# Max-unpooling on one core: inputs and outputs in three sections of whole images, six loads in place of three

## The chip, the cores and the metric

The kernel runs on one core of one Trainium2 chip. The metric is the device time in microseconds of one execution. Ten executions of the kernel before gave a median of 71.7 us, from 71.55 to 71.92. A profiled execution also has a span, from its first recorded instruction to its last.

## The reference

Each input pixel goes to one of the four places of its 2x2 block in an output of twice the height and width; the index, 0 to 3, says which. The other three are zero.

```python
# x: (16, 64, 32, 32) float32; indices: the same shape, values 0..3; kernel_size 2
output = np.zeros((batch, channels, 64, 64), dtype=np.float32)
for b, c, i, j in every position of x:
    idx = indices[b, c, i, j]
    output[b, c, 2 * i + idx // 2, 2 * j + idx % 2] = x[b, c, i, j]
```

(The loop is written in one line here.) On the chip the indices are 64-bit integers in HBM, so that x is 4.19 MB, the indices 8.39 MB and the output 16.78 MB.

## The kernel before, in words

There are 1024 images (batch times channels) of 1024 pixels. Each of the 128 partitions takes eight neighbouring images, `T = 8`. Input and output tiles are laid out by partition: a partition's x is 32 KB in one piece of HBM, its indices 64 KB, its output 128 KB.

Three loads are issued on SP's queue: all of x (L109), then the indices of images 0 to 2 of each partition (24 KB per partition) and those of images 3 to 7 (40 KB; both L112). `Program.first` takes each out of the place where it was made and puts it just ahead of SP's first drain, which is ahead of the barrier at which the engines start together. One semaphore per load tells VectorE of its arrival.

VectorE does all the arithmetic with one kind of instruction (L133): for each of the four places of a block it compares the low 32-bit word of the index (every second word of the tile) with 0, 1, 2 or 3, multiplies the outcome by x, and writes with a step of two pixels in each direction into the output tile. Four such instructions make one or two images per partition. The waits are at L117 (x) and L122 (indices, ahead of images 0 and 3). One or two images are done at a time: 0 and 1, 2, 3, 4 and 5, 6 and 7.

The output goes out in four groups of two images per partition, each 4.19 MB (L146): in HBM a store is 128 pieces of 32 KB, one per partition, 128 KB apart. SP waits for VectorE's count `made`, issues the store, and goes to the next. There are three output tiles; the fourth group uses the first tile again, so that VectorE waits for the first store (L128) ahead of it. At the end of the program SP waits for the other three stores (L151).

All transfers go through one queue in the order of their issue: three loads, then four stores.

Of the kernel before, what the change touches and what calls it, by code (L numbers as in the profile page):

```python
# [1 line left out]

# [4 lines left out]

P = 128
F32 = mybir.dt.float32
I32 = mybir.dt.int32  # L10


class Program:

    def __init__(self, nc):
        self.nc = nc
        self.block = nc.main_func.blocks[0]  # L20
        self.kernel_block = nc.cur_bb.bb.name

    def __enter__(self):
        ins = self.block.instructions
        self.branches = [i for i in ins if "Branch" in type(i).__name__]
        n = len(ins) - len(self.branches)
        assert all("Branch" in type(ins[k]).__name__ for k in range(n, len(ins)))
        del ins[n:]
        self.nc.switch_bb(self.block.name, parent=None)
        self.symbolic = self.nc._always_lower_symbolic_ap  # L30
        self.nc._always_lower_symbolic_ap = False
        return self

    def first(self, made):
        ins = self.block.instructions
        assert ins[len(ins) - 1].name == made.ins.name
        moved = ins.pop()
        at = next(
            k
            for k, i in enumerate(ins)  # L40
            if i.engine == moved.engine and isinstance(i, mybir.InstDrain)
        )
        ins.insert(at, moved)

    def last(self, made):


        def move(nc):
            ins = self.block.instructions
            at = next(k for k, i in enumerate(ins) if i.name == made.ins.name)  # L50
            nc.main_func.blocks[-1].instructions.append(ins.pop(at))

        self.nc.at_finalize(move)

    def __exit__(self, kind, *_):
        self.nc._always_lower_symbolic_ap = self.symbolic
        if kind is None:
            for b in self.branches:
                self.block.instructions.append(b)
            self.nc.switch_bb(self.kernel_block, parent=None)  # L60


@with_exitstack
def kernel(
    ctx: ExitStack,
    tc: tile.TileContext,
    x: bass.AP,
    indices: bass.AP,
    kernel_size: bass.AP,
    out: bass.AP,  # L70
):
    nc = tc.nc
    assert kernel_size == 2

    B, C, H, W = x.shape
    n_img = B * C
    T = n_img // P
    assert T * P == n_img and C % T == 0

    G = 2  # L80
    NG = T // G
    FIRST = 3
    N = H * W
    x_v = x.rearrange("b (ch t) h w -> (b ch) (t h w)", t=T)
    idx_v = indices.rearrange("b (ch t) h w -> (b ch) (t h w)", t=T).bitcast(I32)
    out_v = out.rearrange("b (ch g t) oh ow -> g (b ch) (t oh ow)", g=NG, t=G)

    x_t = nc.alloc_sbuf_tensor("x_t", [P, T * N], F32).ap()
    idx_t = nc.alloc_sbuf_tensor("idx_t", [P, T * 2 * N], I32).ap()
    out_t = [  # L90
        nc.alloc_sbuf_tensor(f"out_t{g}", [P, G * 4 * N], F32).ap()
        for g in range(NG - 1)
    ]
    out_t.append(out_t[0])

    x_in = nc.alloc_semaphore("x_in")
    idx_in = [nc.alloc_semaphore(f"idx_in{g}") for g in range(2)]
    made = nc.alloc_semaphore("made")
    stored_0 = nc.alloc_semaphore("stored_0")
    stored = nc.alloc_semaphore("stored")  # L100

    x_c = x_t.rearrange("p (t i j) -> p t i j", t=T, j=W)
    idx_c = idx_t.rearrange("p (t i j two) -> p t i j two", t=T, j=W, two=2)[
        :, :, :, :, 0
    ]
    cut = FIRST * 2 * N

    with Program(nc) as program:
        program.first(nc.sync.dma_start(out=x_t, in_=x_v).then_inc(x_in, 16))  # L109
        for half, part in enumerate((slice(0, cut), slice(cut, None))):  # L110
            program.first(
                nc.sync.dma_start(out=idx_t[:, part], in_=idx_v[:, part]).then_inc(  # L112
                    idx_in[half], 16
                )
            )

        nc.vector.wait_ge(x_in, 16).then_inc(x_in, -16)  # L117
        for t in range(T):
            g, k = t // G, t % G
            if t in (0, FIRST):  # L120
                half = int(t == FIRST)
                nc.vector.wait_ge(idx_in[half], 16).then_inc(idx_in[half], -16)  # L122

            if k == 1 and t != FIRST:
                continue
            n = 1 if k == 1 or t + 1 == FIRST else 2
            if g == NG - 1:
                nc.vector.wait_ge(stored_0, 16).then_inc(stored_0, -16)  # L128
            o_c = out_t[g].rearrange(
                "p (m i two j wo) -> p m i two j wo", m=G, two=2, wo=2, j=W  # L130
            )
            for pidx in range(4):
                op = nc.vector.scalar_tensor_tensor(  # L133
                    out=o_c[:, k : k + n, :, pidx // 2, :, pidx % 2],
                    in0=idx_c[:, t : t + n],
                    scalar=pidx,
                    in1=x_c[:, t : t + n],
                    op0=mybir.AluOpType.is_equal,
                    op1=mybir.AluOpType.mult,
                )  # L140
            if k + n == G:
                op.then_inc(made, 1)

        for g in range(NG):
            nc.sync.wait_ge(made, g + 1)
            nc.sync.dma_start(out=out_v[g], in_=out_t[g]).then_inc(  # L146
                stored if g else stored_0, 16
            )
        nc.sync.sem_inc(made, -NG)
        program.last(  # L150
            nc.sync.wait_ge(stored, 16 * (NG - 1)).then_inc(stored, -16 * (NG - 1))  # L151
        )


# [1 line left out]
_INS = ['x', 'indices', 'kernel_size']  # L156
_OUTS = [((16, 64, 64, 64), 'float32')]

_NUMBERS = {'kernel_size': 2}


# [26 lines left out]
```

## Time and profile before

| What | Value |
|---|---|
| Median of ten executions | 71.7 us |
| The profiled execution | 71.78 us |
| Its span | 70.5 us |
| VectorE busy | 35.6 us, 20 instructions |
| Of these, 128x2048 | 12, of 2287 ns each |
| Of these, 128x1024 | 8, of 1220 ns each |
| First VectorE instruction of L133 | at 19.75 us |
| SP's issue of the loads | 0.37 us (x), 0.90 us for the two of the indices |
| First and last store issued | at 28.7 and 55.4 us |
| Moved by DMA | 29.36 MB in 1008 packets |

A "packet" is what one DMA engine records as one piece of work. The 1008 are seven transfers on 16 engines with nine packets each: eight of data and a last one of four bytes that counts up the semaphore. The time from issue to landing counts the wait behind earlier transfers of the queue. The profile's chain of work that ended last goes through the engines' instructions; transfers are not steps of it. Lines are those of the kernel printed above.

### The profile page before, as it was taken

What the parts mean: (1) busy time and instruction counts of PE and PEld (TensorE: products, weight loads), DVE (VectorE), ACT (ScalarE), POOL (GpSimd) and SP (SyncE); (2) the same over time, 40 slices, a digit from 0 to 9 for tenths busy, and PEclk for the clock granted to TensorE, in tenths of its full rate; (3) what the DMA queues carried; (4) which work ended last, traced back from release to release, by engine and by line L of the source; (5) the groups of instructions that cost most, each with busy time, mean ns of one, the idle gap of its engine ahead of it and who ended that gap; (6) DMA issues with size and microseconds to landing.
All of it is one profiled execution on the core that took longest, in us unless ns stands there. A gap on an engine that the chain in (4) does not pass through costs nothing.

```text
span 70.5 us, 72 instructions
## 1 busy us (share of the span) xinstructions
DVE 35.6 (51%) x20; POOL 0.2 (0%) x4
## 2 busy tenths in 40 slices
DVE  0000000000079999999999999999999400000000
POOL 1000000000000000000000000000000000000000
DMA  9779796999988999969899897979798998979790
GB/s 260 316 335 539 335 558 274 446 446 446 581 372 372 395 558 488 419 298 521 372 465 428 353 540 316 558 335 539 335 521 372 465 428 353 540 316 558 335 539 37
DMA packets 1009, 29.36 MB, mean 417 GB/s; under 512 B 113, under 2 KB 113, under 8 KB 113
## 3 DMA queue, kind: packets, MB, share of 16 engines
q1 hardware_dynamic: 1008, 29.36, 97.5%
q14 instruction: 1, 0.00, 0.0%
HBM read 12.58 MB, written 16.78 MB: 417 GB/s over the span
## 4 chain that ended last, share of the span: by engine, by line
DVE 46%; DVEq 4%; issue 1%
DVE out_t L133 46%; DVEq L183 4%
## 5 line engine op out<-in xcount | busy, mean ns | idle before, releaser
L133 DVE SCALAR_TENSOR_TENSOR out_t<-idx_t,x_t 128x2048 f32<-128x2048 int32 (+1 forms) x20 | 35.6, 1860 | 19.8 <-DVEq L122 19.8
L169 POOL MEMSET const-bfloat16-1.0<- 128x1 bf16 x1 | 0.1, 101 | 0.0
L169 POOL MEMSET const-uint8-127<- 128x1 uint8 x1 | 0.1, 101 | 0.0
L169 POOL MEMSET const-float32-0.0<- 128x1 f32 x1 | 0.1, 98 | 0.2 <-issue 0.2
L169 POOL MEMSET const-float32-1.0<- 128x1 f32 x1 | 0.1, 98 | 0.0
## 6 DMA issues: line engine op xcount, KB each, us to landing
out_dram<-out_t SPq DMA_DIRECT2D x4, 4096.0 KB, 13.8
idx_t<-in_indices_dram SPq DMA_DIRECT2D x1, 5120.0 KB, 30.9
x_t<-in_x_dram SPq DMA_DIRECT2D x1, 4096.0 KB, 12.3
idx_t<-in_indices_dram SPq DMA_DIRECT2D x1, 3072.0 KB, 19.2
```

The costliest lines, as they stand in the source:

```text
L133: op = nc.vector.scalar_tensor_tensor(out=o_c[:, k : k + n, :, pidx // 2, :, pidx % 2], in0=idx_c[:, t : t + n], scalar=pidx, in1=x_c[:, t ...
L169: nc = _bacc.Bacc("TRN2", target_bir_lowering=False, num_devices=1)
L183: with _tile.TileContext(nc) as tc:
```

## The change

The images are cut in three sections of 256, 384 and 384. In a section a partition takes 2, 3 or 3 neighbouring images, so that a section of x, of the indices or of the output is one unbroken piece of HBM. Each section has a load of x and one of the indices, and one semaphore for both. The six loads are made in the order x0, idx0, x1, idx1, x2, idx2 and placed by `Program.first`. Each section has one store: 4.19, 6.29 and 6.29 MB.

`Program.first` gets `rows_per_read`. With a value above 1 the source of the load is rewritten so that one read spans the rows of several partitions (they follow each other in HBM), while the destination stays as it was, with one row per partition; the mark `ant_dge_precooked` of the instruction is cleared. The values are 1, 4 and 4 for x and 2 for all indices. So the reads are 8, 48 and 48 KB for x and 32, 48 and 48 KB for the indices, and the rows that are written 8, 12 and 12 KB and 16, 24 and 24 KB.

Inputs lie in one tile, section after section. The output tiles of sections 0 and 1 are their own; that of section 2 lies over the inputs of sections 0 and 1. VectorE works on a whole section with four instructions: twelve in all, four of 128x2048 and eight of 128x3072. The wait for the first store goes; ahead of section 2 VectorE waits for `made` to be 2. SP waits for all three stores at the end.

```diff
-    def first(self, made):
+    def first(self, made, rows_per_read=1):
         ins = self.block.instructions
         assert ins[len(ins) - 1].name == made.ins.name
         moved = ins.pop()
+        if rows_per_read > 1:
+            (src,) = moved.ins
+            (step, rows), (one, n) = src.ap
+            assert step == n and one == 1 and rows % (16 * rows_per_read) == 0
+            assert 4 * n * rows_per_read <= bass.MAX_DMA_LAST_DIM
+            n *= rows_per_read
+            wide = copy.replace(src, ap=[[n, rows // rows_per_read], [1, n]])
+            moved = copy.replace(moved, ins=[wide], ant_dge_precooked=False)
         at = next(
...
-    G = 2
-    NG = T // G
-    FIRST = 3
-    x_v = x.rearrange("b (ch t) h w -> (b ch) (t h w)", t=T)
-    idx_v = indices.rearrange("b (ch t) h w -> (b ch) (t h w)", t=T).bitcast(I32)
-    out_v = out.rearrange("b (ch g t) oh ow -> g (b ch) (t oh ow)", g=NG, t=G)
+    SECTIONS = (2, 3, 3)
+    X_ROWS = (1, 4, 4)
+    IDX_ROWS = (2, 2, 2)
...
+    inputs = nc.alloc_sbuf_tensor("inputs", [P, sum(SECTIONS) * 3 * N], F32).ap()
     out_t = [
-        nc.alloc_sbuf_tensor(f"out_t{g}", [P, G * 4 * N], F32).ap()
-        for g in range(NG - 1)
+        nc.alloc_sbuf_tensor(f"out_t{s}", [P, n * 4 * N], F32).ap()
+        for s, n in enumerate(SECTIONS[:-1])
     ]
-    out_t.append(out_t[0])
+    out_t.append(inputs[:, : SECTIONS[-1] * 4 * N])
...
-        program.first(nc.sync.dma_start(out=x_t, in_=x_v).then_inc(x_in, 16))
-        for half, part in enumerate((slice(0, cut), slice(cut, None))):
-            program.first(
-                nc.sync.dma_start(out=idx_t[:, part], in_=idx_v[:, part]).then_inc(
-                    idx_in[half], 16
-                )
-            )
+        for s, n in enumerate(SECTIONS):
+            imgs = slice(img, img + n * P)
...
+            for tile_, hbm, rows in (
+                (x_t[s], x_i, X_ROWS[s]),
+                (idx_t[s], idx_i, IDX_ROWS[s]),
+            ):
+                program.first(
+                    nc.sync.dma_start(
+                        out=tile_, in_=hbm[imgs].rearrange("(p t) n -> p (t n)", t=n)
+                    ).then_inc(arrived[s], 16),
+                    rows_per_read=rows,
+                )
+            out_v.append(out_i[imgs].rearrange("(p t) n -> p (t n)", t=n))
...
+        for s, n in enumerate(SECTIONS):
+            nc.vector.wait_ge(arrived[s], 32).then_inc(arrived[s], -32)
+            if s == NS - 1:
+                nc.vector.wait_ge(made, s)
...
-            if g == NG - 1:
-                nc.vector.wait_ge(stored_0, 16).then_inc(stored_0, -16)
...
-        program.last(
-            nc.sync.wait_ge(stored, 16 * (NG - 1)).then_inc(stored, -16 * (NG - 1))
-        )
+        for s in range(NS):
+            nc.sync.wait_ge(made, s + 1)
+            nc.sync.dma_start(out=out_v[s], in_=out_t[s]).then_inc(stored, 16)
+        nc.sync.sem_inc(made, -NS)
+        program.last(nc.sync.wait_ge(stored, 16 * NS).then_inc(stored, -16 * NS))
```

## The prediction

> **What bounds the kernel now.** I read the page first, then the stretches of the DMA view, the chain, the waits and the issues.
>
> From the page: the span, the DMA queue and the bytes.
>
> ```profile
> span 70.5 us, 72 instructions
> DVE 35.6 (51%) x20; POOL 0.2 (0%) x4
> ...
> q1 hardware_dynamic: 1008, 29.36, 97.5%
> ...
> HBM read 12.58 MB, written 16.78 MB: 417 GB/s over the span
> ```
>
> VectorE is busy for half the span. The one DMA queue keeps its 16 engines busy for 97.5% of it, about 68.7 of 70.5 us. The stretches say when (columns: stretch, its length, VectorE and GpSimd busy, clock, DMA share, GB/s; a packet is booked whole where it starts, so a share can pass 1):
>
> ```profile
> 0.00:0.90 0.90, 0.00 (x0) 0.20 (x4) 1.00 0.00 0
> 0.90:2.00 1.10, 0.00 (x0) 0.00 (x0) 1.00 1.71 477
> 2.00:2.70 0.70, 0.00 (x0) 0.00 (x0) 1.00 0.00 0
> 2.70:3.60 0.90, 0.00 (x0) 0.00 (x0) 1.00 1.35 583
> 3.60:3.90 0.30, 0.00 (x0) 0.00 (x0) 1.00 0.00 0
> 3.90:4.80 0.90, 0.00 (x0) 0.00 (x0) 1.00 1.35 583
> ...
> 68.00:68.90 0.90, 0.00 (x0) 0.00 (x0) 1.00 1.35 583
> 68.90:69.30 0.40, 0.00 (x0) 0.00 (x0) 1.00 0.00 0
> 69.30:70.20 0.90, 0.00 (x0) 0.00 (x0) 1.00 0.01 0
> ```
>
> 583 GB/s for 0.9 us is 525 KB: sixteen packets of 32 KB, one per engine. The share gives their length: 1.35 x 0.9 = 1.21 us. The first sixteen took 1.71 x 1.1 = 1.88 us, that is 0.67 us of waiting for the first data. After that every engine starts a packet each 1.21 us up to 68.9, and the completion packets go out at 69.3 to 70.2. The packet records say it closer: 24, 32 and 40 KB take 912, 1213 and 1514 ns, so 8192 B cost 301 ns (27.2 B/ns per engine), and one engine's 32 KB packets start 1209.5 ns apart, which is 4.8 ns over 32768 / 27.2. No packet after the first has a longer time: no engine starves or waits for HBM.
>
> The chain of work that ended last and the waits show why that is the bound:
>
> ```profile
> 31.98 9.55 DVE out_t L133 x7
> 41.52 0.22 issue
> 41.74 2.60 DVEq L183
> 44.34 11.01 DVE out_t L133 x5
> ```
>
> ```profile
> SPq L146 <- DVE out_t L133: 52.6, 4, 27.0
> SPq L151 <- SPq L151: 14.0, 1, 14.0
> ```
>
> The chain stops at VectorE's last instruction (55.35 us) and does not follow the transfers; the 14.0 us that SP waits after the last store is the rest. Each store is issued before the queue needs it: the first at 28.7 us, when loads still run to 31.4; the last at 55.4, when the one before it runs to about 60.4. The issues say the same: a store is 9.7 us of transfer but lands 13.8 us after its issue.
>
> ```profile
> out_dram<-out_t SPq DMA_DIRECT2D x4, 4096.0 KB, 13.8
> idx_t<-in_indices_dram SPq DMA_DIRECT2D x1, 5120.0 KB, 30.9
> ```
>
> So the span is a start, the bytes of one engine, and an end. One engine moves 29.36 MB / 16 = 1.835 MB: 67.46 us at 27.2 B/ns, plus 63 packets (56 of data, 7 completions) x 0.0048 = 0.30: 67.76. The slowest engine's last completion packet starts at 70.08, so its effective start is 70.08 - 67.76 = 2.32; the semaphore needs another 0.36 to SP. In sum 2.32 + 67.76 + 0.36 = 70.44 of 70.46 us.
>
> **What the Trainium skill says.** "DMA: Bandwidth & Descriptors", section "Where 436 GB/s comes from": 16 ports of 32 B at 850 MHz, 435.2 GB/s. The trace agrees: 16 x 27.2. The same page, "Why small descriptors are slow (HBM only)": about 3 cycles per packet, an estimate of 3.5 ns at 850 MHz; the trace has 4.8. Its section on why a DMA increments its semaphore by 16: the number of engines is the largest up to 16 that divides the slowest dimension of both sides. The trace has 16 with 128 against 128; 64 or 32 against 128 also gives 16, which no run here shows yet. "The descriptor swizzle": each engine writes the partitions of one SBUF port in a 128-partition transfer. The even 1213 ns fits, but the trace names no partition.
>
> **The change part by part.**
>
> Bytes: none added or removed, the same 67.46 us on each engine.
>
> Loads, three to six, in order x0, idx0, x1, idx1, x2, idx2. They are still put ahead of SP's drain, as now; the part of the description about six register instructions is not in the diff, so nothing is booked for it. On the write side each load is 8 packets per engine: 48 in place of 24. On the read side it is 8+4+2+4+2+4 = 24, as now. Stores go from four to three: 24 packets in place of 32. Completions 7 to 9. If the 4.8 ns are paid per write, 81 - 63 = +18, +0.09 us; if per read, 57 - 63 = -6, -0.03 us. The trace has only packets whose two sides are equal, so it can't tell. I take a value between, nearer the first: +0.05.
>
> Issue: three more load issues on SP. Now they take 0.37 to 0.43 us. Five have a cleared mark (ant_dge_precooked) and unequal sides; their price is unknown, from 0.43 up. Cover: x0's eight packets of 8 KB keep each engine busy to 2.32 + 65536 / 27200 = 4.7 us. idx0 is issued at 0.42, and packets now follow the end of an issue by 0.6 us, so its issue may take up to 3.7 us before the engines run dry. At 0.43 to 1 us per issue SP finishes all six by 2.5 to 5.5 us. Behind them wait SP's drain and the start barrier, which VectorE needs only when section 0 has landed. Cost nothing; with the cover gone, one for one.
>
> VectorE: 4 x 2.29 for section 0, and by the slope of the two forms (2.287 - 1.220 = 1.067 us per 1024 elements) 8 x 3.35 for the others: 36.0 us as against 35.6. Section 0 lands at 2.32 + 3.146 MB / 16 / 27.2 = 9.5, +0.3: VectorE runs 9.8 to 19.0. Section 1 lands at about 20.7 and is made by 34.1; section 2 is all there at 31.9 and is made by 47.5. The queue asks for the stores at about 31.5, at 41.2 (store 0 is 262144 B per engine, 9.7) and at 55.7 (store 1 393216 B, 14.5). They are issued 12, 7 and 8 us before that. Nothing is late.
>
> The wait for the first store before its buffer is used again (2.6 us on VectorE in the chain at most) goes; section 2 writes over inputs that VectorE has read. It lay under the stores, so it is worth nothing. The wait on "made" that replaces it asks for what VectorE itself has done. The last wait still counts 48.
>
> Sum against the profiled execution: 70.46 + 0.05 = 70.5 span, and 71.78 + 0.05 = 71.83 with the 1.3 us around it. That execution lay 0.08 above the median of the ten, so the forecast on the median is **71.75 us**.
>
> **The rivals.**
>
> Slower: the widened loads. A 48 KB read that feeds four 12 KB writes must be cut at each write, and if such a write costs a completion packet's own 9 ns on top, 40 writes x 9 = 0.36 + 0.09, 72.15 us. It decides once a write of an unequal load costs above 4.8 + (0.143 - 0.09) / 40 = 6.1 ns. Against it: the trace shows engines bound by bytes, with 99.6% of a 32 KB packet at the full rate. The far end: unequal sides make the generator give each engine partitions of two ports. Two engines at one port halve the loads' rate: 11.53 MB / 16 / 27.2 = +26 us, 98 us. The division by four rows fits a group of four partitions, so I think that rare.
>
> Faster: the start. All engines pay 0.67 us for the first data, and they are spread over 0.76 us from then on to the end (the sixteen starts fill 2.7 to 3.6 as they do 68.0 to 68.9), the slowest setting the end. The first load now has 8 KB rows, so that the engines begin 32 KB apart in HBM rather than 128 KB. If they came as evenly as their middle, some 0.4 us go: 71.35. Against it: the load's 128 descriptors and its queue are unchanged[...].
>
> VectorE as the bound, or a starved queue between stores: it would need section 1 or 2 to be 7 us late; I give it nothing of its own. That the contiguous pieces speed HBM up: the packets already run at the port's rate; worth nothing.
>
> **How the numbers follow.** A difference of 0.2%, 0.14 us, is about what a measurement of this kernel can tell from none. Bytes bind, little changed: 0.50, of it 0.41 same, 0.06 slower, 0.03 faster (own range 71.55 to 71.95). Widened loads slower: 0.29, of it 0.03 past 73 us. Start quicker, or packets paid per read with luck: 0.21, of it 0.03 within the bound. Faster 0.21, same 0.44, slower 0.35. The range goes from 71.35 (the whole start rival) to 72.4 (twice the slower rival's price for a write); what is left out is port sharing and a slow issue.
>
> **What would show it.** Right: packets of one engine back to back from 2 to 70 us, the queue's share near 97.5%, DVE's first start near 9.8 us, its end near 47.5, and SP's last wait some 22 us. Wrong: loads that land later than 32 us, a packet of an unequal load that takes more than bytes / 27.2 + 9 ns, a gap before store 0, or first packets that come earlier or closer together than 2.7 to 3.6 us.

## The result and the profile after

The changed kernel takes 72.77 us (median; 72.68 to 73.17), the kernel before 71.66 us. The ratio is 1.0165, interval 1.0151 to 1.0179: slower by 1.1 us. The forecast was 71.75 us, range 71.35 to 72.4.

The page after: span, VectorE, queue and bytes.

```profile
span 71.4 us, 65 instructions
...
DVE 35.2 (49%) x12; POOL 0.2 (0%) x4
...
q1 hardware_dynamic: 912, 29.36, 97.3%
HBM read 12.58 MB, written 16.78 MB: 411 GB/s over the span
```

The span grew by 0.9 us, while bytes are the same and VectorE even a little less busy. The queue's share is still 97%, so that the lost time must lie inside what the engines record as work. There are 912 packets and not 1008: 57 per engine, the count that the prediction had for "per read". A wide read is recorded as one packet, 48 KB for instance.

VectorE after (start, length, what, and in brackets the idle time before it), and SP's last wait:

```profile
9.97 8.90 DVE L149 SCALAR_TENSOR_TENSOR out_t<-inputs 128x2048 f32<-128x2048 int32 x4 [9.97 <-DVEq L138]
20.96 13.17 DVE L149 SCALAR_TENSOR_TENSOR out_t<-inputs 128x3072 f32<-128x3072 int32 x4 [2.10 <-DVEq L138]
34.16 13.16 DVE L149 SCALAR_TENSOR_TENSOR inputs<-inputs 128x3072 f32<-128x3072 int32 x4
```

```profile
SPq L163 <- SPq L163: 23.0, 1, 23.0
```

VectorE starts at 9.97 us and ends at 47.3, as forecast (9.8, 47.5); SP's last wait is 23.0 us, forecast some 22. Only the transfers came out otherwise. The stretches after and then before, in the columns of the prediction's stretches:

```profile
27.00:28.00 1.00, 1.00 (x2) 0.00 (x0) 1.00 1.83 786
29.00:30.00 1.00, 1.00 (x1) 0.00 (x0) 1.00 2.76 786
31.60:32.40 0.80, 0.80 (x1) 0.00 (x0) 1.00 1.53 655
```

```profile
29.00:30.00 1.00, 1.00 (x2) 0.00 (x0) 1.00 1.51 655
30.50:31.40 0.90, 0.90 (x2) 0.00 (x0) 1.00 1.36 583
```

786 GB/s in 1 us is sixteen packets of 48 KB. Those that start in 27 to 28 us take 1.83 us each. The next sixteen, which start in 29 to 30 us, take 2.76: 0.93 us more. They are the last packets of the last load (idx2). After them come the first packets of store 0, from 31.6 to 32.4, and from there the engines run evenly to the end. Before, the same place had no such thing: the last sixteen packets of 40 KB took 1.51 us (the stretch from 29 to 30), like all of their size, and the first packets of the first store follow from 30.5 to 31.4. So nearly the whole loss is one stall, at the turn from loads to stores.

From the packet records, per engine, what its packets take over bytes / 27.2 + 9 ns: before 0.64 us, all in the first packets; after 1.52, of it 0.43 in the packets that start by 2 us, 0.94 in the last packets of the loads, and the rest, 0.15, in the seam behind x0 and in the widened reads.

SP's queue of the changed kernel (start, length, what) shows when the loads and store 0 were issued. The line with x2 runs from the issue of the first store to the end of the issue of the second:

```profile
0.00 0.37 SPq L128 DMA_DIRECT2D inputs<-in_x_dram  x1
0.43 0.53 SPq L128 DMA_DIRECT2D inputs<-in_indices_dram  x1
...
2.96 0.59 SPq L128 DMA_DIRECT2D inputs<-in_indices_dram  x1
18.90 15.60 SPq L161 DMA_DIRECT2D out_dram<-out_t  x2
```

The widened loads take 0.53 to 0.63 us to issue, within what the prediction allowed. Store 0 is issued at 18.9 us; before, at 28.7:

```profile
28.68 0.35 SPq L146 DMA_DIRECT2D out_dram<-out_t  x1
```

### The profile page after: what moved, and what is told of

It reads as the page before. It is cut to its first block, busy times and chain, and to the rows that moved or that the text cites. A ratio compares the mean times of both kernels' runs of the same rounds, so it can differ in the third digit from the quotient of the medians.

```text
span 71.4 us, 65 instructions
## 1 busy us (share of the span) xinstructions
DVE 35.2 (49%) x12; POOL 0.2 (0%) x4
## 3 DMA queue, kind: packets, MB, share of 16 engines
q1 hardware_dynamic: 912, 29.36, 97.3%
## 5 line engine op out<-in xcount | busy, mean ns | idle before, releaser
L149 DVE SCALAR_TENSOR_TENSOR out_t<-inputs 128x2048 f32<-128x2048 int32 (+1 forms) x8 | 22.1, 2821 | 12.1 <-DVEq L138 12.1
L149 DVE SCALAR_TENSOR_TENSOR inputs<-inputs 128x3072 f32<-128x3072 int32 x4 | 13.2, 3353 | 0.0
```

The lines of the kernel that those rows point to most:

```text
L149: op = nc.vector.scalar_tensor_tensor(out=o_c[:, :, pidx // 2, :, pidx % 2], in0=idx_c, scalar=pidx, in1=x_c, op0=mybir.AluOpType.is_equal ...
```

## The experiments

The first theory was the one that the trace suggests first: the wide reads, new and right at the place of the stall.

**Wide reads taken back.** All six loads with equal sides:

```diff
-    X_ROWS = (1, 4, 4)
-    IDX_ROWS = (2, 2, 2)
+    X_ROWS = (1, 1, 1)
+    IDX_ROWS = (1, 1, 1)
```

> All six loads read one row per partition (equal sides); sections, order and stores as in the changed kernel. Theory A (the wide reads make the stall at the turn from loads to stores): the last load packets take 912 ns per 24 KB without the 0.94 us on top, the span falls from 71.4 to about 70.2, the time to 71.4 to 71.6, at or below the kernel before (71.66). Rival B (the stores that are queued 12 us early, or the sections being one piece of HBM, make it): the stall stays, 72.6 to 72.9.

Measured 72.89 us, ratio 1.0166 (1.0138 to 1.0194). Theory A falls. The stall now lies on the last two packets of 24 KB (stretches of this run):

```profile
29.00:30.00 1.00, 1.00 (x1) 0.00 (x0) 1.00 1.42 393
30.00:31.00 1.00, 1.00 (x2) 0.00 (x0) 1.00 1.23 344
```

393 GB/s in 1 us is sixteen packets of 24 KB at 1.42 us, the next fourteen take 1.23 x 16 / 14 = 1.41; they need 0.91. Again it is the last 48 KB of each engine.

**Only the last load narrow, and only the last load wide.** `IDX_ROWS = (2, 2, 1)` in the one; `X_ROWS = (1, 1, 1)`, `IDX_ROWS = (1, 1, 2)` in the other.

> Only the last load, idx2, reads one row per partition; the other four stay wide. Theory A1 (only a wide load that stands right before a store stalls): no stall, 71.4 to 71.7. Theory A2 (any wide load followed by one with equal sides stalls): the stall moves to the end of x2, ahead of idx2, and 72.6 to 72.9 stays. Rival B: the stall stays where it is.

> Only the last load, idx2, reads two rows at once; the other five have equal sides. Theory A1: the whole stall is there, 72.5 to 72.8. Were the cost spread over all wide loads, a third or less of the 1.1 us would be left: 71.6 to 72.0.

Measured 72.95 us, 1.016 (1.0125 to 1.0194), and 72.91 us, 1.0168 (1.0138 to 1.0198). In both the stall is at the turn. The second agrees with A1 in its time, but with the first run beside it that says nothing for the wide load: the stall is there whichever loads are wide.

**A small first load in the kernel before.** This tests the prediction's rival of the start.

```diff
-        program.first(nc.sync.dma_start(out=x_t, in_=x_v).then_inc(x_in, 16))
+        for part in (slice(0, 2 * N), slice(2 * N, None)):
+            program.first(
+                nc.sync.dma_start(out=x_t[:, part], in_=x_v[:, part]).then_inc(x_in, 16)
+            )
...
-        nc.vector.wait_ge(x_in, 16).then_inc(x_in, -16)
+        nc.vector.wait_ge(x_in, 32).then_inc(x_in, -32)
```

> The kernel before, with its load of x cut in two: images 0 and 1 of each partition (8 KB rows, 32 KB apart), then images 2 to 7. Theory S (a small first packet lets the engines start closer together): the sixteen first packets end within 0.35 us and not 0.76, and the time falls by 0.2 to 0.4 us to 71.3 to 71.5. Rival (the start depends on where the engines begin in HBM, which is unchanged here): start and time as before, 71.6 to 71.8.

Measured 71.53 us against 71.71, ratio 0.998 (0.997 to 0.999). The gain is real and about half of what was expected. The sixteen first packets take 0.41 us over their bytes and not 0.67, but they do not end closer together: they end between 1.39 and 2.44 us. So the theory is right in its direction and not in its reason. This version is faster than both kernels, by 0.2% than the kernel before. The 0.41 is of one profile. Over all the profiles of this document with a first load of 8 KB rows the same figure goes from 0.23 to 0.68 us (14 kernels, middle 0.42), over the three with 32 KB rows from 0.60 to 0.67.

**Early store or one piece of HBM?** With the reads out, the two remaining differences at the turn were the moment at which store 0 is queued and the layout in HBM. Store 0 was made later by letting an earlier VectorE instruction of section 1 count `made`, and the waits on `made` moved up by one:

```diff
+                if s == 1 and pidx == 1:
+                    op.then_inc(made, 1)
             op.then_inc(made, 1)
...
-            nc.sync.wait_ge(made, s + 1)
+            nc.sync.wait_ge(made, s + 2)
```

(`pidx == 0` in the second such run.) In a third run the sections, the narrow loads and the early stores stay, but the images are dealt out as before:

```diff
-    x_i = x.rearrange("b ch h w -> (b ch) (h w)")
+    x_i = x.rearrange("b (ch t) h w -> (b ch) (t h w)", t=T)
...
-                        out=tile_, in_=hbm[imgs].rearrange("(p t) n -> p (t n)", t=n)
+                        out=tile_, in_=hbm[:, img * w : (img + n) * w]
```

(idx_i, out_i and out_v likewise; `w` is the words of an image, `img` counts images of a partition.)

> The changed kernel with the first store issued after the second of section 1's four instructions, at about 27.6 us (some 3 us before the loads end, as in the kernel before) in place of 18.9. Theory Q (the stall comes from the store that is queued 12 us ahead of its turn): no stall at 29 to 31 us, 71.4 to 71.8. Theory C (the store or the loads being one piece of HBM): the stall of 0.94 us stays, 72.6 to 72.9.

> As the run with the late first store, but issued after the first of section 1's instructions, at about 24.3 us, some 7 us before the loads end. Theory Q: a stall between none and 0.94 us, 71.5 to 72.7. Theory C: the whole stall, 72.6 to 72.9.

> Three sections, six loads with equal sides, three stores, stores queued as early as in the changed kernel, but the images of a partition are its eight neighbours as in the kernel before: a section is 128 pieces, one per partition, at a pitch of 32 KB (x), 64 KB (indices) and 128 KB (output). Theory C: no stall at the turn, 71.3 to 71.7. Theory Q: the stall stays, 72.6 to 73.0.

Measured 72.78 us, 1.0161 (1.0133 to 1.0189), with store 0 at 27.34; 72.89 us, 1.0169 (1.0147 to 1.0192), at 24.21; and 72.72 us, 1.0146 (1.0129 to 1.0164), with the pitched sections. Neither theory fits: the layout is out, and a store eight us later seemed to change nothing.

**Back to the kernel before, from the other side.** Its last load was cut to 24 KB packets, and then all its loads were cut, to six; and three of VectorE's four instructions per section were taken out of the changed kernel.

```diff
-        program.first(nc.sync.dma_start(out=x_t, in_=x_v).then_inc(x_in, 16))
-        for half, part in enumerate((slice(0, cut), slice(cut, None))):
+        for a, b in ((0, 2), (2, 5), (5, 8)):
+            part = slice(a * N, b * N)
...
+        for a, b, half in ((0, 3, 0), (3, 5, 1), (5, 8, 1)):
+            part = slice(a * 2 * N, b * 2 * N)
```

(The first loop makes the loads of x, the second those of the indices; in the first of the two runs x stays one load. The waits count the additional loads; those lines are left out here.)

> The kernel before with its last load of the indices cut in two, 16 and 24 KB per partition: four loads, the last as in the changed kernel. Theory L (the stall depends on the size of the last load's packets): a stall of about 0.9 us at 29 to 31 us, 72.4 to 72.7. Theory N (it grows with the number of loads or packets ahead of the turn): little or none with 36 packets per engine, 71.5 to 71.9. Theory D (VectorE's instructions at the time of the turn): none, 71.5 to 71.8.

> The kernel before with x cut in three loads (8, 12 and 12 KB per partition) and the indices in three (24, 16 and 24 KB): six loads with 54 packets per engine, as the changed kernel on its write side, but all of x ahead of the indices, and VectorE and the stores as before. Theory N: the stall of 0.9 us is there, 72.3 to 72.7. Theory L: likewise. Theory D, or the order of the loads, or the larger stores: no stall, 71.3 to 71.6.

Measured 71.81 us, 1.0013 (1.0001 to 1.0025), and 71.71 us, 1.0008 (0.9998 to 1.0017). Theories L and N fall; the second run has 0.07 us at the turn, the first none.

```diff
+        for t in out_t[:-1]:
+            nc.vector.memset(t, 0.0).then_inc(zeroed, 1)
+        nc.vector.wait_ge(zeroed, NS - 1).then_inc(zeroed, 1 - NS)
...
-            for pidx in range(4):
+            for pidx in range(1):
```

> The changed kernel with one of the four instructions per section (the places 1 to 3 of each block are left out; the output tiles of sections 0 and 1 are zeroed at the start instead), so that VectorE is nearly idle at the turn. Theory D (VectorE's work at the turn makes the stall): no stall, 71.4 to 71.8. Theories L and N: the stall stays, 72.5 to 73.0.

Measured 71.85 us, 1.0039 (0.9987 to 1.0091), and 0.03 us at the turn. That looks like theory D. But VectorE was not idle there after all, as this run's trace shows; the zeroing held it up:

```profile
15.35 10.30 DVE L139 MEMSET out_t<- 128x12288 f32 x1 [2.51 <-issue]
25.91 5.56 DVE L153 SCALAR_TENSOR_TENSOR out_t<-inputs 128x2048 f32<-128x2048 int32 x2 [0.26 <-DVEq L142]
28.23 3.61 SPq L165 DMA_DIRECT2D out_dram<-out_t  x2
```

It ran a 128x3072 instruction, the second of the two in the line at 25.91, through the turn. What was moved is store 0, to 28.23 us. Set beside 27.34 (stall) and 28.7 (kernel before, none), that asks for a threshold between.

**The moment of the store, three times.** Section 1's second and third instruction are cut into one per image, which gives finer moments; store 0 is counted at one of them, (1, 2, 0) for 28.8 us and (1, 1, 2) for 27.6. The waits on `made` move up by one as above. And the kernel before gets its first store early, by cutting its first load of the indices in two, so that VectorE can start on images 0 and 1 (with a third semaphore for the indices).

```diff
+                cuts = (0, 1, 2, 3) if s == 1 and pidx in (1, 2) else (0, n)
+                for a, b in zip(cuts, cuts[1:]):
...
+                    if (s, pidx, a) == (1, 2, 0):
+                        op.then_inc(made, 1)
```

```diff
-        for half, part in enumerate((slice(0, cut), slice(cut, None))):
+        for half, part in enumerate(
+            (slice(0, 4 * N), slice(4 * N, cut), slice(cut, None))
+        ):
...
-            if t in (0, FIRST):
-                half = int(t == FIRST)
+            if t in (0, 2, FIRST):
+                half = (0, 2, FIRST).index(t)
```

> The changed kernel, with the second and third of section 1's four VectorE instructions cut into one per image, and the first store issued after the first image of the third: about 28.8 us. Theory Q2 (the stall comes when the store is in the queue before the engines have begun their last 48 KB of loads, at about 29.0 to 29.5 us): no stall, span about 70.5, time 71.6 to 71.9. Theory D (VectorE's work at the turn): the stall stays, 72.6 to 73.0.

> The same cut instructions, the first store issued after the last image of the second, about 27.6 us. Theory Q2: the stall of about 0.94 us stays, 72.6 to 73.0. If the smaller instructions removed the stall, 71.6 to 71.9.

> The kernel before, with its first load of the indices cut in images 0 and 1 and image 2, so that VectorE begins at about 17 us and the first store is issued at about 26.3 us in place of 28.7, some 4.5 us before the loads end. Four loads, all with the bytes and places of before. Theory Q2: a stall of about 0.9 us appears in the last 40 KB packets, 72.3 to 72.8. Theory D, or anything of the sections: no stall, 71.5 to 71.9.

Measured: at 28.81 us 71.75 us, 1.0008 (0.9998 to 1.0017), span 70.4; at 27.57 us 72.83 us, 1.0156 (1.0136 to 1.0176); the kernel before with its store at 26.02 us 72.7 us, 1.0143 (1.0119 to 1.0166). All three as theory Q2 had it. The changed kernel with the store at 28.81, its issue and the stretch with the last load packets:

```profile
28.81 5.88 SPq L165 DMA_DIRECT2D out_dram<-out_t  x2
```

```profile
29.00:30.00 1.00, 1.00 (x2) 0.00 (x0) 1.00 1.49 639
30.00:31.00 1.00, 1.00 (x2) 0.00 (x0) 1.00 0.38 164
31.00:32.00 1.00, 1.00 (x2) 0.00 (x0) 1.00 0.99 426
```

The kernel before with its store at 26.02:

```profile
26.02 29.33 SPq L148 DMA_DIRECT2D out_dram<-out_t  x4
```

```profile
29.00:30.00 1.00, 1.00 (x2) 0.00 (x0) 1.00 2.50 655
30.00:31.00 1.00, 0.54 (x1) 0.00 (x0) 1.00 0.00 0
31.00:32.00 1.00, 0.00 (x0) 0.00 (x0) 1.00 0.76 328
```

In the first, 639 GB/s is thirteen of the sixteen packets of 48 KB, at 1.49 x 16 / 13 = 1.83 us: no stall. In the second, sixteen packets of 40 KB take 2.50 us and not 1.51: the same stall, in a kernel with none of the sections, wide reads or large stores, and with VectorE idle for part of it.

**The window, and the wide reads without the stall.** The store one instruction later (`(1, 2, 1)`), and the store at 28.8 with all reads narrow.

> As the run with the store at 28.8 us, one VectorE instruction later: about 29.9 us. The store's packets need some 1 us to reach the engines, which are free at 30.6 to 31.3. If only the early store costs, no stall in the loads, and a gap of up to 0.3 us on the engines that are free first, none on the slowest: 71.6 to 71.9, as at 28.8. If the window is narrow on this side too: 72.0 to 72.5.

> As the run with the store at 28.8 us, with all reads of one row (equal sides, 81 packets per engine in place of 57). Wide reads save packets and cost 10 to 30 ns per read in the trace: the two nearly cancel, 71.65 to 71.85. If the wide reads gain what they save in packets (24 x 5 ns and no cost): 71.85 to 71.95. If they cost: 71.5 to 71.65.

Measured 71.77 us, 1.0017 (1.0008 to 1.0027), with the store at 29.90; and 71.79 us, 1.001 (1.000 to 1.002), span 70.5. A store that is issued only 0.8 us ahead of the first engine's turn takes some 0.1 us more than the kernel before, 0.2 at the far end of the interval; its first packet starts 0.09 us after its engine is free (packet records). Wide reads gain or lose nothing that these runs can tell.

All kernels by the moment of store 0 (the stall is the time of the last load packets over bytes / 27.2 + 9 ns, per engine, from the packet records):

| Store 0 issued, us | Kernel | Stall, us |
|---|---|---|
| 18.7 to 18.9 | changed; three with other reads; pitched sections | 0.85 to 1.07 |
| 24.21 | changed, later store | 0.99 |
| 26.02 | before, earlier store | 0.99 |
| 27.34, 27.57 | changed, later store | 0.94, 0.98 |
| 28.23 | changed, one place only | 0.03 |
| 28.53, 28.57, 28.59 | before with more loads | 0.00, 0.05, 0.07 |
| 28.68 | before | 0.00 |
| 28.81, 28.83, 29.90 | changed, later store | 0.01, 0.00, 0.01 |

In the kernels without the stall the first engine ends its loads at 30.6 to 30.9 us and the last at 31.2 to 31.4 (packet records). They issue store 0 between 0.8 and 2.6 us ahead of the first engine's turn. The latest store that stalls, at 27.57, is 3.2 us ahead of it: an estimate, since the stall moved that turn; it takes the first start of a last load packet in that run, 28.98, and 1.83 us for the packet.

## Why the prediction was wrong

**The step that failed** is the last sentence of the paragraph on VectorE: the stores are issued 12, 7 and 8 us ahead of the queue's demand, "Nothing is late." It asked only whether a store comes late. A store that comes early was booked at nothing, and its price is 0.94 us in the mean of the engines. In time it is 1.08 us between the two runs that differ in nothing but the store's moment (71.75 us at 28.81, 72.83 at 27.57). The sum "a start, the bytes of one engine, and an end" has no term for the turn from loads to stores, because the trace of before showed none; it showed none because its store came at 28.7 us: with the store at 26.02 the same kernel has the stall. The part on what bounds the kernel read the moment of 28.7 us as a proof of slack, where it also was a condition.

**The rival on the slow side** had the sign, and its place was close: it looked at the widened loads, and the stall lies on them in the profile. One of its signs even appeared, a packet of an unequal load far above bytes / 27.2 + 9 ns (2.76 us). But its mechanism is refuted: reads all narrow, the stall is the same (72.89 us); reads wide with a late store, it is gone (71.75 us). So its sign was luck. A write of an unequal load costs far less than the 9 ns named: the wide reads' whole excess per engine, some 0.1 us, is 2.5 ns for each of the 40 writes, and about what they save in packets. Port sharing did not happen: a 48 KB packet of a widened load took 1.83 us.

**The start rival** came true in small part. The first packets' excess in the changed kernel is 0.43 us per engine as against 0.67, and in the kernel before a small first load gave 0.998. The prediction gave up to 0.4 us; that run gained some 0.15 to 0.2. In the changed kernel no gain shows in the total, not even without the stall: 1.0008, 1.0017 and 1.001 in the three versions with a late store. What takes it up there is open.

**What held**: the bytes at 27.2 B/ns per engine; loads' issue under cover (0.53 to 0.63 us); VectorE's times. That the wait for the first store's buffer is worth nothing fits the trace of before, in which VectorE's only recorded wait is the one at its start (19.8 us, L122). Packets are counted per read, where the prediction leaned to per write; the two lay 0.12 us apart. Two small slips changed nothing: section 2 is all there at 31.5 us by the prediction's own sum and not 31.9, and three of the later 32 KB packets of before are longer than the others (1.254 us at most in place of 1.213). With the store issued at 28.8 us the changed kernel takes 71.75 us, which is the forecast to the digit; that says that the other terms were right in sum, in part by luck since the shorter start does not show, and not that the forecast was right.

**What stays open** is why. Shown is the condition, by the moment of issue. With the same VectorE instructions the store at 27.57 us brings the stall and at 28.81 does not, and an earlier first store brings it into the kernel before. It lies on the last 40 to 48 KB that each engine loads, and it is no larger if the store is queued ten us earlier, so that it is not the act of issuing that disturbs the loads. What happens inside the engines no run shows. All transfers here go through SP's queue; whether a store on another queue would do the same was not tried.

## What to carry to other kernels

When loads and stores share a queue and the transfers are the bound, look at the packets on both sides of the turn from loads to stores, and try the first store at several moments: too early can cost as well, here 1.1 us. The stores that cost little or nothing were issued 0.8 to 2.6 us ahead of the first engine's turn; a result that was ready earlier did best to wait. No run came late enough to say what lateness costs. A difference that stays when each suspected feature is undone one by one may hang on something that none of these edits moves far enough, here the moment of one transfer.

## What the runs showed of the hardware that was not expected

- A store queued behind loads on the same queue stalls the loads' last 40 to 48 KB per engine by 0.85 to 1.07 us when it is issued 27.57 us or earlier, and by 0 to 0.07 when it is issued at 28.23 or later, with the turn at about 30.6 to 31.4 us. Between 27.57 and 28.23 nothing was tried.
- The stall is recorded as longer load packets, so that the queue's busy share (97.3% as against 97.5%) does not show it.
- Reads that span two or four rows, with writes of one row, run on 16 engines at the same rate to within about 2%: 1.83 us for 48 KB in a widened load, 1.815 in a store (packet records).
- The kernel before gained 0.2% (0.1 to 0.3) by a first load of 8 KB rows in place of 32 KB. The engines' wait for first data fell from 0.67 to 0.41 us in that profile, but it varies from 0.23 to 0.68 between kernels with the same small first rows.
